# A hybrid decoder layer on one core: a head's norm moved into the next head, value products two steps behind their transposes, and the input norm on VectorE alone

## The chip, the cores and the metric

The kernel runs on one core of a Trainium2 chip, as one launch. The metric is the device time of that core in microseconds (us), taken as the median over the runs of a kernel. A profiled execution gives the trace; its span is the time from the first to the last instruction, and its own device time is a little longer.

## What is computed

One layer over S = 512 rows of D = 2048 float32 numbers. The input is RMS-normalised, multiplied by one wide weight matrix, and its columns feed two branches whose outputs are merged by per-channel gates, projected and added to the input; a last RMS norm follows.

```
xn   = x * rsqrt(mean(x*x) + eps) * norm_w
proj = xn @ w_in                     # queries, keys, values, gates of both branches
# branch 1: HGRN2, 8 heads of 128, o_t = S_t^T q_t
#   S_t = diag(f_t) S_(t-1) + (1 - f_t) i_t^T;  each head's o: rmsnorm(o, hg_norm_w) * silu(z)
# branch 2: native sparse attention, 16 heads of 128 in 4 groups
#   o = g0 * softmax(q kc) vc  +  g1 * softmax(q k_slc) v_slc  +  g2 * softmax(q k_win) v_win
y    = g * (o_hg @ w_branch_hg) + (1 - g) * (o_nsa @ w_branch_nsa)
out  = rmsnorm(x + y @ w_out, final_norm_w)
```

The heads' norm (the mean over the 128 rows of a head, `rmsnorm(o, hg_norm_w)`), the input norm and the attention's weighted sum of values are what the change touches. The compressed keys and values (kc, vc) are 31 blocks per group.

## The kernel before, in words

All large products are three TensorE products in a 32-bit format (`mm3`, lines 139 to 141): each float32 operand is split into a rounded high part and the rest. The split takes one cast on ScalarE and one subtraction on VectorE: `load_w` (lines 130 and 131) for weights that DMAs bring in blocks of 512 KB on SyncE's queue, `split` (lines 135 and 136) for everything computed.

A planner orders each engine's instructions from the written order, with the buffers' reuse as constraints; an engine then runs its queue in that order, and waits where an operand or a buffer isn't ready. `weave(main, n, side, m)` (line 272) interleaves two generators: main yields between the products of a weight matrix, and side steps in proportion m to n.

PSUM, the memory that TensorE writes, has eight banks: three `pj` for projections, two `sc`, two `pt` and one `po`; `lbank` (line 95) takes `sc` and `pt` in turn.

The stages, by their place in the span: the input norm, transposes of x and the first products (0 to 61 us); gate units and column sums (to 125); gates and values (to 475); the eight recurrence heads (475 to 860); the compressed keys and values and the first branch's output (to 1160); the four groups of the sparse attention, NSA (1160 to 1700); the second branch's and the output products (to 2107).

*Input norm.* `normalise(i)` (line 323) takes one of four row tiles: squares of one half on ScalarE (line 329) and of the other on VectorE (line 330), the sum (line 335), root (336), reciprocal (337). Of the four quarters of 512 columns two are scaled and multiplied by the norm's weight in one VectorE operation, STT (line 341: tensor times scalar times tensor); the other two are first multiplied by the weight on GpSimd (line 334) and then scaled on VectorE (line 343). GpSimd also spreads the weight over the partitions (line 305). `transposed` (349) and `first` follow per quarter.

*Recurrence heads.* `hg_proj(h + 1)` is woven with 17 steps of `hg_core(h)` (line 540). The core builds decayed queries and keys by levels of halved blocks: `grow` (line 567) and `decayed` (line 577) on VectorE with a product on GpSimd (566), TensorE's scores (587, 601) and masked copies on VectorE (588, 590, 605). Then transposes of kd (635, copied to kn), state updates (TensorE 644, VectorE 648), the output products in `po` (655, 657), its squares, and at the end the norm: two products with a matrix of 1/128 (668, 669), root (670), reciprocal (671), STT (672), the product with the gate (673), and a store to `ohg_d`.

*NSA groups.* `nsa_proj(g + 1)` (queries, keys, two gate units `z_units`) is woven with `nsa_core(g)` (line 849). The values of a group come from DRAM by two DMAs on ScalarE's queue into a tile of their own, `vraw`, of one buffer (line 822), which is split into vh and vl. `nsa_core` starts with the compressed scores of four heads (copied, transposed at 868, softmaxed in `pc` by lines 876 to 885); `cmp_t` (line 892) transposes the result into pch and pcl. Per head and per block of rows i = 3 to 0 come the scores (in `sc` banks, evacuated by line 921 with mask and maximum), the exponential (925), and the scaling on GpSimd (930). Then, per part, transposes of the probabilities (949), their split into pth and ptl, and the value products of the part before, in `po`.

## Time and profile before

| | |
|---|---|
| median of 3 runs | 2109.39 us (2108.59 to 2112.3) |
| profiled execution, its own time | 2108.82 us |
| its span | 2106.7 us |
| TensorE busy | 98% of the span |
| VectorE busy | 57% |
| ScalarE busy | 39% |
| GpSimd busy | 15% |
| mean granted clock of TensorE | 0.996 |

TensorE's busy share says that it nearly always has a product in its pipeline; it does not say that it starts one at its best pace, since a product that waits a little is hidden behind the one before. What a wait costs is read from the starts of its products and from the table of waits.

### The profile page before, as it was taken

The page shows a single profiled execution, that of the slowest core. Times are in us where ns is not written, and L with a number is a line of the kernel's source. Part 1 is how long each engine was busy: PE and PEld are TensorE (multiplying, and loading weights), DVE is VectorE, ACT ScalarE, POOL GpSimd, SP SyncE. Part 2 cuts the span into 40 slices and gives each one's busy share as a digit, 9 for nine tenths or more (in the row PEclk, how much of TensorE's full clock was granted, in tenths as well). Part 3 has the DMA queues.
Part 4 walks back from the last instruction along what each step waited for, and adds up shares of the span by engine and source line. Part 5 has one row for each costly group of instructions (what it writes and reads, how often), then busy time and mean ns, then how long its engine had stood idle before and what let it go on. Part 6 is the DMA issues. An engine that isn't in the chain of part 4 may idle for free.

```text
span 2106.7 us, 26671 instructions
## 1 busy us (share of the span) xinstructions
PE 2062.0 (98%) x10304; PEld 1721.2 (82%) x10304; DVE 1209.0 (57%) x1875; ACT 816.5 (39%) x1267; POOL 322.4 (15%) x411
## 2 busy tenths in 40 slices
PE   7999999999999999999999999999999999999998
PEld 6888888888888778878888887877878888888887
DVE  7687778745456655566545665657654453433333
ACT  4454444532233233344323444445445432222232
POOL 2000000003233432100002222213212100000000
PEclk9999999999999999999999999999999999999999
DMA  6325243332323222566752222222223394445232
GB/s 184 100 105 180 100 152 114 121 101 74 96 83 93 76 76 85 167 188 202 247 164 85 74 73 85 68 84 64 78 75 92 90 304 132 149 140 212 98 130 90
DMA packets 306595, 254.46 MB, mean 121 GB/s; under 512 B 10666, under 2 KB 263411, under 8 KB 305827
## 3 DMA queue, kind: packets, MB, share of 16 engines
q1 hardware_dynamic: 282980, 202.55, 31.8%
q0 software_dynamic: 8096, 26.28, 3.4%
q10 hardware_dynamic: 15392, 23.92, 3.3%
q8 instruction: 81, 1.33, 0.3%
q14 instruction: 46, 0.38, 0.1%
HBM read 222.25 MB, written 30.47 MB: 120 GB/s over the span
## 4 chain that ended last, share of the span: by engine, by line
PE 82%; DVE 7%; issue 4%; ACT 3%; DMA 3%; POOL 1%; SPq 0%; ACTq 0%; DVEq 0%; POOLq 0%
PE pj L139 17%; PE pj L141 17%; PE pj L140 17%; PE sc L214 4%; PE pt L214 4%; PE sc L215 2%; PE pt L215 2%; PE sc L141 2%; PE sc L139 2%; PE sc L140 2%; PE po L140 1%; DVE whl L131 1%; PE po L139 1%; PE po L141 1%; PE pt L949 1%
## 5 line engine op out<-in xcount | busy, mean ns | idle before, releaser
L139 PE MATMUL pj<-xhl,whl 128*128 128x512 f32 x1344 | 538.5, 401 | 0.0
L141 PE MATMUL pj<-xhl,whl 128*128 128x512 f32 x1344 | 527.7, 393 | 0.8 <-DVE whl L131 0.8
L140 PE MATMUL pj<-xhl,whl 128*128 128x512 f32 x1344 | 525.2, 391 | 0.0
L131 DVE TENSOR_TENSOR whl<-wr,whl 128x1024 fp32r<-128x1024 f32 x244 | 303.8, 1245 | 373.2 <-ACT whl L130 372.5
L130 ACT CAST whl<-wr 128x1024 fp32r<-128x1024 f32 x244 | 256.5, 1052 | 563.3 <-PE pj L141 446.8
L141 PEld LDWEIGHTS pj<-xhl,whl 128*128 128x128 f32 x1344 | 252.3, 188 | 56.6 <-DVE whl L131 2.0
L140 PEld LDWEIGHTS pj<-xhl,whl 128*128 128x128 f32 x1344 | 252.9, 188 | 46.4
L139 PEld LDWEIGHTS pj<-xhl,whl 128*128 128x128 f32 x1344 | 252.7, 188 | 46.1
L135 ACT CAST whl<-xt 128x1024 fp32r<-128x1024 f32 x75 | 78.6, 1052 | 97.7 <-PE pt L215 33.1
L136 DVE TENSOR_TENSOR whl<-xt,whl 128x1024 fp32r<-128x1024 f32 x75 | 91.5, 1223 | 39.3 <-ACT whl L135 39.2
L930 POOL TENSOR_SCALAR s<-s,sm 128x512 f32<-128x512 f32 (+3 forms) x128 | 82.2, 655 | 149.4 <-DVE sm L928 89.9
L139 PE MATMUL pj<-onh,whl 128*128 128x512 f32 x256 | 99.6, 389 | 0.0
L140 PE MATMUL pj<-onl,whl 128*128 128x512 f32 x256 | 99.6, 389 | 0.0
L141 PE MATMUL pj<-onh,whl 128*128 128x512 f32 x256 | 99.6, 389 | 0.0
L136 DVE TENSOR_TENSOR ptl<-pt,pth 128x512 fp32r<-128x512 f32 (+1 forms) x80 | 50.5, 633 | 69.3 <-ACT pth L135 68.6
L925 ACT ACTIVATE s<-s,mx 128x512 f32<-128x512 f32 (+3 forms) x128 | 70.9, 555 | 43.8 <-DVE mx L923 39.0
L135 ACT CAST pth<-pt 128x512 fp32r<-128x512 f32 (+1 forms) x80 | 43.5, 544 | 96.1 <-PE pt L949 95.7
L201 DVE TENSOR_TENSOR xt<-xt 128x1024 f32<-128x1024 f32 x64 | 77.5, 1219 | 0.6
L921 DVE CUSTOM_DVE_ANT_0 s<-sc,cf 128x512 f32<-128x512 f32 (+3 forms) x128 | 59.3, 483 | 20.1 <-PE sc L141 19.4
L698 POOL TENSOR_TENSOR rsh<-rsh,rope 32x512 f32<-32x512 f32 x28 | 42.2, 1507 | 183.8 <-DVE rsh L697 166.3
L566 POOL TENSOR_TENSOR suf<-suf,pre 128x256 f32<-128x256 f32 x56 | 51.8, 926 | 116.7 <-DVE pre L549 94.6
L131 DVE TENSOR_TENSOR cl<-wr,ch 128x1024 fp32r<-128x1024 f32 x32 | 39.1, 1223 | 44.6 <-ACT ch L130 44.6
(431 smaller groups left out, 4004.9 us busy)
## 6 DMA issues: line engine op xcount, KB each, us to landing
wr<-in_w_in_dram SPq DMA_DIRECT2D x172, 512.0 KB
xt<-in_w_in_dram SPq DMA_DIRECT2D x32, 1024.0 KB
wr<-in_w_branch_nsa_dram SPq DMA_DIRECT2D x32, 512.0 KB
wr<-in_w_out_dram SPq DMA_DIRECT2D x32, 512.0 KB
wr<-in_cmp_k_w_dram SPq DMA_DIRECT2D x16, 512.0 KB
wr<-in_w_branch_hg_dram SPq DMA_DIRECT2D x16, 512.0 KB
wr<-in_cmp_v_w_dram SPq DMA_DIRECT2D x16, 512.0 KB
gat_d<-wr POOLq DMA_DIRECT2D x20, 256.0 KB, 3.0
```

The source lines that it names most:

```text
L130: nc.scalar.copy(hi[:, :n], raw[:, :n])
L131: nc.vector.tensor_tensor(lo[:, :n], raw[:, :n], hi[:, :n].bitcast(F32), op=OP.subtract)
L135: nc.scalar.copy(hi, src)
L136: nc.vector.tensor_tensor(lo, src, hi.bitcast(F32), op=OP.subtract)
L139: nc.tensor.matmul(acc, lhsT=lh, rhs=rh, start=start, stop=False, **kw)
L140: nc.tensor.matmul(acc, lhsT=lh, rhs=rl, start=False, stop=False, **kw)
L141: nc.tensor.matmul(acc, lhsT=ll, rhs=rh, start=False, stop=stop, **kw)
L201: nc.vector.tensor_tensor(dst, dst, more, op=OP.add)
L214: nc.tensor.matmul(av, lhsT=l0, rhs=r, start=start, stop=False, skip_group_check=True)
L215: nc.tensor.matmul(av[:, 0], lhsT=l1, rhs=r[:, 0], start=False, stop=stop, skip_group_check=True)
L925: nc.scalar.activation(s[:, b], s[:, b], AF.Exp, scale=SCALE, bias=mx[:, b:b + 1], accum_out=sm[:, b:b + 1])
L930: nc.gpsimd.tensor_scalar(s[:, b], s[:, b], sm[:, b:b + 1], 1.0, op0=OP.mult, op1=OP.mult)
```

## The change

Three edits. In `normalise` all four quarters use the one VectorE operation, and GpSimd's products go. In `hg_core` the norm of a head becomes a function that is kept in a list and run in the next head, after that head's kn; the last head runs its own at its end. In the NSA, the values are loaded in two tiles named `raw` (two buffers, shared with the roped queries and keys, the gate units and the compressed values); the value products wait in a list `due` until two steps after their transposes, and the last two of a head run in the next head's score steps; the first score product of block 2 goes to a `pj` bank; `cmp_t` comes right after the scores of block 1 of the first head; pth384 and ptl384 have two buffers; the weave takes 46 steps and not 48.

```diff
             nc.scalar.activation(sq, x[:, h1], AF.Square, accum_out=ss[:, 1:2])
             nc.vector.scalar_tensor_tensor(sq2, x[:, h0], 1.0, x[:, h0], op0=OP.mult, op1=OP.mult,
                                            accum_out=ss[:, 0:1])
-            for k0 in (8, 12):
-                c = slice(k0 * P, (k0 + 4) * P)
-                nc.gpsimd.tensor_tensor(x[:, c], x[:, c], nw[:, c], op=OP.mult)
             nc.vector.tensor_tensor(ss[:, :1], ss[:, :1], ss[:, 1:], op=OP.add)
             nc.scalar.activation(ss[:, :1], ss[:, :1], AF.Sqrt, scale=1.0 / D, bias=epst)
             nc.vector.reciprocal(ss[:, :1], ss[:, :1])
             for k0 in range(0, KD, 4):
                 c = slice(k0 * P, (k0 + 4) * P)
-                if k0 < 8:
-                    nc.vector.scalar_tensor_tensor(x[:, c], x[:, c], ss[:, :1], nw[:, c], op0=OP.mult, op1=OP.mult)
-                else:
-                    nc.vector.tensor_scalar(x[:, c], x[:, c], ss[:, :1], None, op0=OP.mult)
+                nc.vector.scalar_tensor_tensor(x[:, c], x[:, c], ss[:, :1], nw[:, c], op0=OP.mult, op1=OP.mult)
 
         def transposed(i, k0):
             ts = slice(i * P, (i + 1) * P)
...
     with pool("hg") as hp:
         hgw = sv[:, R_HGW:R_HGW + 1]
         heads = {}
+        left = []
         def values(pr):
 
             vb = [bank() for _ in range(2)]
...
             kn = hp.tile([P, 3 * P], F32, name="kn", bufs=2)
             nc.scalar.copy(kn, ps[:, :3 * P])
             yield
+            if left:
+                left.pop()()
             yield
             ps = lbank()
             st = hp.tile([P, 3, P], F32, name="st", bufs=2)
...
             split(sh, sl, ob)
             yield
             yield
-            pm = lbank()
-            nc.tensor.matmul(pm, lhsT=ones, rhs=sh, start=True, stop=False)
-            nc.tensor.matmul(pm, lhsT=ones, rhs=sl, start=False, stop=True)
-            nc.scalar.activation(ob, pm, AF.Sqrt, bias=epst)
-            nc.vector.reciprocal(ob, ob)
-            nc.vector.scalar_tensor_tensor(ow, ow, hgw, ob, op0=OP.mult, op1=OP.mult)
-            nc.vector.tensor_tensor(ow, ow, zs, op=OP.mult)
-            nc.gpsimd.dma_start(ohg_d[head], ow)
+
+            def normed():
+                pm = lbank()
+                nc.tensor.matmul(pm, lhsT=ones, rhs=sh, start=True, stop=False)
+                nc.tensor.matmul(pm, lhsT=ones, rhs=sl, start=False, stop=True)
+                nc.scalar.activation(ob, pm, AF.Sqrt, bias=epst)
+                nc.vector.reciprocal(ob, ob)
+                nc.vector.scalar_tensor_tensor(ow, ow, hgw, ob, op0=OP.mult, op1=OP.mult)
+                nc.vector.tensor_tensor(ow, ow, zs, op=OP.mult)
+                nc.gpsimd.dma_start(ohg_d[head], ow)
+
+            left.append(normed)
+            if head == HG - 1:
+                left.pop()()
 
         weave(hg_proj(0), 0)
         for head in range(HG - 1):
...
     gv5 = gt.rearrange("p i (g h b) -> p i g h b", g=GROUPS, b=3)
 
     def nsa_proj(g):
-        raw = ap.tile([P, 4, 2, DH], F32, name="vraw")
-        for b in range(2):
-            nc.scalar.dma_start(raw[:, :, b], v_d[1 + b, :, :, g * DH:(g + 1) * DH].rearrange("i p c -> p i c"))
         vh = ap.tile([P, 4, 2, DH], F32R, name="vh", bufs=2)
         vl = ap.tile([P, 4, 2, DH], F32R, name="vl", bufs=2)
-        f = lambda t: t.rearrange("p j e c -> p (j e c)")
-        split(f(vh), f(vl), f(raw))
+        for b in range(2):
+            raw = ap.tile([P, S], F32, name="raw", bufs=2)
+            rv = raw.rearrange("p (i c) -> p i c", i=4)
+            nc.scalar.dma_start(rv, v_d[1 + b, :, :, g * DH:(g + 1) * DH].rearrange("i p c -> p i c"))
+            split(vh[:, :, b], vl[:, :, b], rv)
         q = []
         for h in range(HPG):
             acc = bank()
...
         p3h = ap.tile([P, 2, HPG, P], F32R, name="p3h")
         p3l = ap.tile([P, 2, HPG, P], F32R, name="p3l")
         o3 = ap.tile([P, HPG, P], F32, name="o3")
+        due = []
+
+        def pv_next():
+
+            if not due:
+                return
+            h, po, parts, hi, lo, last = due.pop(0)
+            for n, (j, b) in enumerate(parts):
+                w = slice(n * (4 - j) * P, (n + 1) * (4 - j) * P)
+                mm3(po[:, j * P:], vh[:, j, b], vl[:, j, b], hi[:, w], lo[:, w], False, last)
+            if last:
+                ow = ap.tile([P, 384], F32, name="ow", bufs=2)
+                nc.vector.tensor_copy(ow, po[:, :384])
+                nc.scalar.copy(o3[:, h], po[:, 384:])
+                nc.gpsimd.dma_start(ons_d[g * HPG + h][:, :384], ow)
+
         for h in range(HPG):
             qh, ql = q[h]
             sc = {}
...
                 s = sc[i] = ap.tile([P, 2, n], F32, name=f"s{i}", bufs=1)
                 mx = ap.tile([P, 2], F32, name="mx", bufs=4)
                 sm = ap.tile([P, 2], F32, name="sm", bufs=4)
+                if i > 1:
+                    pv_next()
                 if i < 2:
                     ps = sbank()
                     pv = ps[:, :2 * n].rearrange("p (b k) -> p b k", b=2)
...
                 else:
                     pb = []
                     for b in range(2):
-                        ps = sbank()
+                        ps = bank() if i == 2 and b == 0 else sbank()
                         mm3(ps[:, :n], qh[:, qs], ql[:, qs], kh[:, b, :n], kl[:, b, :n], True, True)
                         pb.append(ps[:, :n])
                 mk = causal[:, 3 - i:].rearrange("p j k -> p (j k)")
...
                 nc.vector.tensor_tensor(sm, sm, gv[:, i, h, 1:3], op=OP.mult)
                 for b in range(2):
                     nc.gpsimd.tensor_scalar(s[:, b], s[:, b], sm[:, b:b + 1], 1.0, op0=OP.mult, op1=OP.mult)
+                if h == 0 and i == 1:
+                    cmp_t()
                 yield
-            if h == 0:
-                cmp_t()
-                yield
-            po = psum("po")
-            mm3(po, vcz[0][:, h], vcz[1][:, h], ph, pl, True, False)
-            pend = None
-
-            def pv_mm(parts, hi, lo, last):
-                for n, (j, b) in enumerate(parts):
-                    w = slice(n * (4 - j) * P, (n + 1) * (4 - j) * P)
-                    mm3(po[:, j * P:], vh[:, j, b], vl[:, j, b], hi[:, w], lo[:, w], False, last)
-
-            for parts in (((3, 0), (3, 1)), ((2, 0), (2, 1)), ((1, 0),), ((0, 0),), ((1, 1),), ((0, 1),)):
+            for m, parts in enumerate((((3, 0), (3, 1)), ((2, 0), (2, 1)), ((1, 0),), ((0, 0),), ((1, 1),), ((0, 1),))):
                 ps = tbank()
                 o = 0
                 for j, b in parts:
...
                     pv = ps[:, :o].rearrange("p (b k) -> p b k", b=2)
                     split(p3h[:, :, h], p3l[:, :, h], pv)
                 else:
-                    hi = ap.tile([P, o], F32R, name=f"pth{o}", bufs=o // 256)
-                    lo = ap.tile([P, o], F32R, name=f"ptl{o}", bufs=o // 256)
+                    hi = ap.tile([P, o], F32R, name=f"pth{o}", bufs=2)
+                    lo = ap.tile([P, o], F32R, name=f"ptl{o}", bufs=2)
                     split(hi, lo, ps[:, :o])
-                    if pend:
-                        pv_mm(*pend, False)
-                    pend = (parts, hi, lo)
+                    if m == 2:
+                        po = psum("po")
+                        mm3(po, vcz[0][:, h], vcz[1][:, h], ph, pl, True, False)
+                    elif m > 2:
+                        pv_next()
+                    due.append([h, None, parts, hi, lo, m == 5])
+                    if m >= 2:
+                        for d in due:
+                            d[1] = po
                 yield
-            pv_mm(*pend, True)
-            ow = ap.tile([P, 384], F32, name="ow", bufs=2)
-            nc.vector.tensor_copy(ow, po[:, :384])
-            nc.scalar.copy(o3[:, h], po[:, 384:])
-            nc.gpsimd.dma_start(ons_d[g * HPG + h][:, :384], ow)
+        while due:
             yield
+            pv_next()
+        yield
 
         ps = sbank()
         for b in range(2):
...
 
     weave(nsa_proj(0), 0)
     for g in range(GROUPS - 1):
-        weave(nsa_proj(g + 1), 128, nsa_core(g), 48)
+        weave(nsa_proj(g + 1), 128, nsa_core(g), 46)
     
     def last():
         yield from z_units(14, 16, ap, "raw")
         yield from merge_gates(NG, NG + 6, ap, "raw")
 
-    weave(last(), 112, nsa_core(GROUPS - 1), 48)
+    weave(last(), 112, nsa_core(GROUPS - 1), 46)
     nsa.close()
 
 
```

The planner's order shows where the pieces come to lie. First VectorE at the start, before and then after (xt is x, wfl the low part of the first weight, xhl the split x):

```order
L341 SCALAR_TENSOR_TENSOR xt<-xt,ss,nw 128x512 x2
L131 TENSOR_TENSOR wfl<-wraw,wfh 128x1216
L136 TENSOR_TENSOR xhl<-pt,xhl 128x4x128
L131 TENSOR_TENSOR wfl<-wraw,wfh 128x1216
L136 TENSOR_TENSOR xhl<-sc,xhl 128x4x128
L330 SCALAR_TENSOR_TENSOR sq_269,ss<-xt 128x1024
L343 TENSOR_SCALAR xt<-xt,ss 128x512 x2
L335 TENSOR_TENSOR ss<-ss 128x1
L337 RECIPROCAL ss<-ss 128x1
```

```order
L337 SCALAR_TENSOR_TENSOR xt<-xt,ss,nw 128x512 x4
L131 TENSOR_TENSOR wfl<-wraw,wfh 128x1216
L136 TENSOR_TENSOR xhl<-pt,xhl 128x4x128
L131 TENSOR_TENSOR wfl<-wraw,wfh 128x1216
L136 TENSOR_TENSOR xhl<-sc,xhl 128x4x128
L136 TENSOR_TENSOR xhl<-pt,xhl 128x4x128
L136 TENSOR_TENSOR xhl<-sc,xhl 128x4x128
L330 SCALAR_TENSOR_TENSOR sq_267,ss<-xt 128x1024
L332 TENSOR_TENSOR ss<-ss 128x1
```

All four quarters of the first tile are scaled before the first weight's subtraction; two splits of x follow the second weight without another row tile between them.

Second VectorE at the end of a head's state updates, from those updates to the next head's first ones: before, and then after (st is the state, ob and ow the norm's tiles, ad the scores, zs the gate):

```order
L648 SCALAR_TENSOR_TENSOR st<-st,pre,sc 128x128 x2
L131 TENSOR_TENSOR whl<-wr,whl 128x1024 x2
L537 TENSOR_TENSOR zs<-pj,zs 128x512
L136 TENSOR_TENSOR sl<-ob,sh 128x512
L131 TENSOR_TENSOR whl<-wr,whl 128x1024 x2
L547 TENSOR_SCALAR kt<-sg,nomlb,omlb 128x512
L549 TENSOR_SCALAR pre<-sg,omlb,lbt 128x512
L552 TENSOR_TENSOR qf<-qf,pre 128x4x64
L671 RECIPROCAL ob<-ob 128x512
L567 TENSOR_TENSOR pre<-pre 128x256
L131 TENSOR_TENSOR whl<-wr,whl 128x1024
L672 SCALAR_TENSOR_TENSOR ow<-ow,sv,ob 128x512
```

```order
L620 TENSOR_TENSOR qd<-qf,pre 128x384
L600 COPY_PREDICATED ad<-cm,sc 128x16x16
L131 TENSOR_TENSOR whl<-wr,whl 128x1024 x2
L670 RECIPROCAL ob<-ob 128x512
L131 TENSOR_TENSOR whl<-wr,whl 128x1024
L671 SCALAR_TENSOR_TENSOR ow<-ow,sv,ob 128x512
L645 SCALAR_TENSOR_TENSOR st<-st,pre,sc 128x128
L672 TENSOR_TENSOR ow<-ow,zs 128x512
L645 SCALAR_TENSOR_TENSOR st<-st,pre,sc 128x128
L532 TENSOR_TENSOR zs<-pj,zs 128x512
```

The reciprocal, STT and product have moved from ahead of the next head's `pre`, `qk` and masked copies to between the qd product, the scores' last copy and the state updates.

Third ScalarE at the start of an NSA group (group 1), before and then after:

```order
L135 CAST vh<-vraw 128x1024
L130 CAST whl<-wr 128x1024
L178 ACTIVATE raw<-pj 128x512
L822 DMA vraw<-v_d 128x4x128
L855 DMA raw<-vc_d 31x128 x4
L864 COPY pc<-sc 128x512
L822 DMA vraw<-v_d 128x4x128
L135 CAST vczh<-raw 128x512
L879 ACT_TABLE_LOAD
L879 ACTIVATE pc<-pc 128x512
```

```order
L130 CAST whl<-wr 128x1024
L178 ACTIVATE raw<-pj 128x512
L828 DMA raw<-v_d 128x4x128
L135 CAST vh<-raw 128x4x128
L867 COPY pc<-sc 128x512
L828 DMA raw<-v_d 128x4x128
L858 DMA raw<-vc_d 31x128 x4
L135 CAST vh<-raw 128x4x128
L882 ACT_TABLE_LOAD
L882 ACTIVATE pc<-pc 128x512
```

The two loads of the values now stand ahead of and behind the copy of the compressed scores, the cast of each half comes right behind, and the exponential stands behind the second cast.

## Rows read from the trace of the kernel before

**Rows 1.** Page, busy time: us, share of span, instructions; first engine.

```profile
PE 2062.0 (98%) x10304; PEld 1721.2 (82%) x10304; DVE 1209.0 (57%) x1875; ACT 816.5 (39%) x1267; POOL 322.4 (15%) x411
```

**Rows 2.** Timeline of TensorE, 584 to 591 us: start, us, line, shape; first and last.

```profile
584.16 0.40 PE L139 MATMUL pj<-xhl,whl 128*128 128x512 f32 x1
...
590.08 0.39 PE L141 MATMUL pj<-xhl,whl 128*128 128x512 f32 x1
```

**Rows 3.** Waits of TensorE, whole span: waited for, us, times, longest.

```profile
PE sc L139 <- DVE mx L921: 8.9, 6, 2.5
PE sc L601 <- DVE ad L605: 7.4, 7, 1.3
...
PE pt L349 <- issue: 3.4, 2, 1.8
PE pt L349 <- DVE xt L343: 1.7, 1, 1.7
...
PE po L140 <- DVE ptl L136: 1.6, 3, 0.5
```

**Rows 4.** Busy time by stretch: length, us busy (instructions), clock, DMA share, GB/s.

```profile
25.50:28.80 3.30, 3.30 (x13) 2.76 (x13) 3.30 (x4) 3.30 (x6) 0.00 (x0) 0.50 0.44 136
30.00:60.00 30.00, 26.85 (x189) 25.08 (x189) 29.54 (x39) 14.25 (x25) 6.33 (x5) 1.00 0.31 83
```

**Rows 5.** Groups by line, GpSimd, 0 to 62 us: busy, mean ns, idle before.

```profile
L334 POOL TENSOR_TENSOR xt<-xt,nw 128x512 f32<-128x512 f32 x8 | 11.6, 1472 | 15.8 <-issue 7.4 <-ACT sq L329 5.6 <-DMA wr<-in_w_in_dram 2.7
```

**Rows 6.** Groups by line and shape, VectorE, 0 to 62 us.

```profile
L343 DVE TENSOR_SCALAR xt<-xt,ss 128x512 f32<-128x512 f32 x8 | 7.5, 974 | 1.9 <-POOL xt L334 1.9
L341 DVE SCALAR_TENSOR_TENSOR xt<-xt,ss,nw 128x512 f32<-128x512 f32 x8 | 5.9, 768 | 2.7 <-POOL nw L305 2.7
...
L335 DVE TENSOR_TENSOR ss<-ss 128x1 f32<-128x1 f32 x4 | 3.7, 925 | 1.7 <-ACT sq L329 1.5
...
L337 DVE RECIPROCAL ss<-ss 128x1 f32<-128x1 f32 x4 | 0.6, 158 | 0.7 <-ACT ss L336 0.7
```

**Rows 7.** Timeline of VectorE, 583 to 602 us: start, us, line.

```profile
598.47 0.72 DVE L605 COPY_PREDICATED ad<-cm,sc 128x256 f32<-128x256 uint8 x1
```

**Rows 8.** Groups by line and shape, VectorE, 475 to 860 us.

```profile
L671 DVE RECIPROCAL ob<-ob 128x512 f32<-128x512 f32 x8 | 26.8, 3346 | 0.7 <-ACT ob L670 0.7
L672 DVE SCALAR_TENSOR_TENSOR ow<-ow,sv,ob 128x512 f32<-128x512 f32 x8 | 9.5, 1192 | 0.0
...
L673 DVE TENSOR_TENSOR ow<-ow,zs 128x512 f32<-128x512 f32 x8 | 6.0, 747 | 0.0
L648 DVE SCALAR_TENSOR_TENSOR st<-st,pre,sc 128x128 f32<-128x128 f32 x16 | 5.6, 348 | 22.3 <-PE sc L644 22.3
```

**Rows 9.** Groups by line and shape, ScalarE, 475 to 860 us.

```profile
L130 ACT CAST whl<-wr 128x1024 fp32r<-128x1024 f32 x55 | 57.8, 1051 | 186.9 <-PE pj L141 186.7
...
L670 ACT ACTIVATE ob<-pt,epst 128x512 f32<-128x512 f32 x8 | 5.5, 691 | 0.1
```

**Rows 10.** Timeline of TensorE, 1291 to 1297 us.

```profile
1295.66 0.60 PE L892 MATMUL pt<-ident,pc 128*128 128x128 f32 x4
```

**Rows 11.** Timeline of VectorE, 1270 to 1294 us.

```profile
1292.00 0.86 DVE L885 TENSOR_TENSOR pc<-pc,cst 128x512 f32<-128x512 f32 x1
```

**Rows 12.** Timeline of ScalarE, 1270 to 1294 us.

```profile
1274.27 0.39 ACTq L822 DMA_DIRECT2D vraw<-v_d  x1
...
1285.44 1.28 ACT L879 ACT_TABLE_LOAD   x1 [2.20 <-DVE pc L878]
1286.73 0.63 ACT L879 ACTIVATE pc<-pc 128x512 f32<-128x512 f32 x1
```

**Rows 13.** Timeline of GpSimd, 1272 to 1292 us.

```profile
1276.27 0.54 POOL L180 DMA_DIRECT2D z_d<-raw  x1 [1.76 <-DVE raw L179]
```

**Rows 14.** DMA issues, 1274 to 1278 us: KB each, us to landing.

```profile
z_d<-raw POOLq DMA_DIRECT2D x1, 256.0 KB, 6.0
```

**Rows 15.** DMA issues of the whole span: KB each, median us to landing.

```profile
v_d<-wr POOLq DMA_DIRECT2D x12, 256.0 KB, 3.5
```

## The prediction

> **What bounds the kernel now.** I read the page first: TensorE is busy 2062.0 of 2106.7 us [rows 1], so a change can only win what TensorE loses between its instructions. A 128x512 product starts every 0.228 us when nothing is in its way (26 steps from 584.16 to 590.08 [rows 2]), and this change neither removes nor adds products for TensorE. So the question is which waits go and which come. The table of TensorE's waits over the whole span [rows 3] gives the candidates; the three edits lie at three places in it, and at each I then read the rows of the engines that are waited for.
>
> - First stage (0 to 62 us). TensorE loses 3.4 us at two transposes of x for which the table names no engine and 1.7 for the scaling of x at line 343 [rows 3]. VectorE is busy 29.54 of the 30 us from 30 to 60 [rows 4]: here it is the bound. GpSimd makes it worse. Its multiplies start 7.4 us late for nothing that the profile shows [rows 5], and while they run VectorE is slow: eight scalings of line 343 take 974 ns in the mean, four one-column adds of line 335 take 925 [rows 6]. The clock is granted at 0.50 (1.2 of 2.4 GHz) from 25.5 to 28.8 [rows 4].
> - Recurrence heads (475 to 860 us). TensorE waits 7.4 us, seven times, at line 601 for the masked copy of line 605 [rows 3]. In the second head that copy starts only at 598.47 [rows 7], since the reciprocal, the scaled product and the product with the gate (3346, 1192 and 747 ns [rows 8]) of the head before stand ahead of it in VectorE's queue. Counted as TensorE's starts against its pace, the seven cost 9.3 us (the table's 7.4 is plain idle time).
> - NSA groups (1140 to 1700 us). TensorE waits 8.9 us in six places for the evacuation of score banks and 1.6 us for the low part of transposed probabilities, ptl [rows 3]. Against its pace I count 11.5 us at the four group starts (0.95, 3.65, 2.95, 3.95) and 2.6 at ptl.
>
> **The change part by part.**
>
> Input norm. Eight scalings of line 343 and eight GpSimd multiplies go; eight more of line 341's operation (STT) come. The scalings take 7.5 us in all; eight STT take 5.9 in all now [rows 6], so 5.9 more. The adds of line 335 take 3.7 us for four and, with GpSimd quiet, should take what the one-column reciprocal takes, 158 ns each [rows 6]: 3.1 less. VectorE also sits idle 1.9 us until GpSimd is done [rows 6]. That is 1.6 + 3.1 + 1.9 = 6.6 us in a stage that VectorE bounds. Against it, the subtraction of the first weight part stands behind two more STT, 1.5 us later; the third part comes earlier, since its cast stands on ScalarE behind a root that waits for a held-up add. I take 5.0 us gained. Bounds: 1 (if the first weight part's delay and a slow clock eat most) and 6.7 (the waits 3.4 + 1.7 [rows 3] and 1.6 for the slow clock, half of 3.3). GpSimd's switch of 7.4 us [rows 5] now falls ahead of its first product of the recurrence stage; between its last work before and that product it has some 24 us of nothing to do, so I cost it at nothing. Without that cover the first head would start as much later.
> Only the means over both states stand in the rows: an STT at 768 ns, a scaling at 974 [rows 6]. The Trainium skill (VectorE: DVE Perf Modes, Mode 2×_2P) says the opposite of fp32: one tensor with a scalar can use both read ports, two tensors cannot, so that the scaling should be the shorter. By that rule alone a scaling takes half of 768 ns and the edit costs VectorE eight times 0.38 us, a loss of 3.1 and not a gain of 1.6. I go by the rows, which have GpSimd beside it.
>
> Late norm of a head. Two products, root, reciprocal, STT, product and the store of ohg_d move from the end of a head to the next one's kn step. The store stays on GpSimd's queue, and nobody reads it before the branch product. The 9.3 us at line 601 should go: without 5.3 us of work (3.35 + 1.19 + 0.75 [rows 8]) ahead of it, the copy is done before TensorE asks. But the moved work now stands ahead of the state updates of line 648 (the second order below: reciprocal, a weight subtraction, STT, one update, product, the other update). Counted from the transposes of kd: products of ones after 2.3 us, root done at 3.1 (0.69 [rows 9]), reciprocal to 6.5; the weight subtraction waits for a cast (1.05 [rows 9]) behind TensorE's last product of a weight block at 6.5, so it runs from 7.5 to 8.7; STT to 9.4 (0.74 when nothing slows it, the nearest being the product's 0.75), first update 0.35 [rows 8] to 9.75. TensorE reaches the product that reads it after 36 products at 0.228 and ten small ones at about 0.1: 9.2. It waits 0.6 us, and 0.5 more for the second update behind the product of 0.75. That is 1.1 us in each of six heads (2 to 7, whose order is the same), 6.6 us. Taken: 9.3 - 6.6 = 2.7 gained. Bounds: 0 (1.5 a head, STT at its mean of 1.19) and 9.3 (no new wait).
>
> NSA. Value products run two steps behind their transposes, so ptl is no longer waited for: 2.6 us gained. The second buffers of pth384 and ptl384, and the bank of the other kind for one score product, cost TensorE nothing: they only take waits away. Two things cost. First, the transposes of the compressed probabilities (cmp_t, line 892) come 12 TensorE instructions earlier. Now they start at 1295.66 [rows 10], after two waits of 3.65 us in all; without waits TensorE would be there at 1292.0, and 12 instructions sooner at 1289.4, while pc is finished at 1292.86 (1292.00 + 0.86 [rows 11]). So TensorE waits 3.4 us even with pc as early as today: the wait changes its name. Second, the load of the values loses its own buffer. Today it is issued at 1274.27 [rows 12], a whole group ahead of its use. After the change its second half shares two buffers with the gate unit, whose store is issued at 1276.27 [rows 13] and lands 6.0 us later [rows 14], at 1282.3. Then come the load (3.5, the median of the stores to v_d of its size [rows 15]), a cast (about 0.6, half of a 128x1024 one [rows 9]), the table load (1.28) and the exponential, at 1287.7; it starts at 1286.73 now [rows 12]. ScalarE's queue holds the exponential behind that cast (third order below), VectorE's five steps on pc hang on it, and TensorE on them. So 3.4 + 0.9 = 4.3 us at each of four starts, 17.2 against 11.5: 5.7 lost, with ptl 3.1 lost. Bounds: 9.1 lost (5.8 each, the load landing 1.5 later) and 14.1 gained (all waits gone: 11.5 + 2.6).
>
> Sum: 5.0 + 2.7 - 3.1 = 4.6 us gained, 2108.82 to 2104.2 for the profiled execution. The median of the runs shown is 0.57 above that execution: **2104.8 us**.
>
> **The rivals.**
> 1. All waits at the group starts go, and the new one in the heads does not show. For it: TensorE's total wait at ptl and sc is there to be won, the loads may be early enough, and the weight cast in the heads hangs on a buffer that may come free sooner. Against it: pc is late today as well [rows 11]. 5.0 + 9.3 + up to 14.1; with half of the last 21.3: 2088. A milder form (new head waits gone, NSA even) gives 14.3: 2095.
> 2. No gain at the start. TensorE has to wait 1.4 us more for the first weight part and some for the next x tiles, and a wait may bring the clock to 0.50 as from 25.5 to 28.8 [rows 4], at 1.7 us. Then 0 + 2.7 - 3.1: 2109.8, no change. The rule above of the Trainium skill (VectorE: DVE Perf Modes, Mode 2×_2P) would lead here.
> 3. Slower: the second half of the values, behind the gate unit's store, holds ScalarE's queue longer. With the load taking 6.0 us (as the store [rows 14]) and not 3.5, the wait is 6.8 each, 27.2: NSA loses 13.1, and 5.0 + 2.7 - 13.1 = -5.4 gives 2114.8. It decides from 6.5 us a start on.
> 4. The change does not do what it says: the planner could put the pieces back where they were. The orders below exclude it.
>
> **How the numbers follow.** The forecast and its neighbours (gains of 0 to 9) have 0.58; rival 1 has 0.20, rival 2 0.12, rival 3 0.10. A measurement of this kernel can tell about 0.2% (4.2 us) from no change, so faster is below 2105.2. Of the forecast's 0.58 a little over half lies beyond it; with rival 1 that makes faster 0.50. Rival 2 and the rest of the forecast make the same 0.38, and rival 3 with a little of rival 2 slower 0.12. The ends of the sum, which need every bound at once: all low, 1 + 0 - 9.1, 2117.5; all high, 6.7 + 9.3 + 14.1, 2079. The range leaves out the far parts of rivals 1 and 3: 2094 to 2113.
>
> **What would show it.** Right: no wait of line 343 in the first stage and the last first-stage product some 5 us earlier than now; no wait at line 601 for line 605; in its place one before the products that read st, about 1 us a head; waits of about 4 us a group start before the transposes of pc, released by the last step on pc, and none for ptl. Wrong: the value load's second half not behind the store, TensorE not stopping at st, or the clock at half for longer in the first stage.

## The result

The changed kernel takes 2085.81 us in the median of four runs (2082.91 to 2087.46), and the one before 2108.99 on the same occasions: a ratio of 0.9887, with a 95% interval of 0.9869 to 0.9905. That is 23 us, 1.1%, where 4.6 us were forecast. The profiled execution took 2082.91 us at a span of 2081.1.

The page of the changed kernel, busy time (before: [rows 1]):

```profile
span 2081.1 us, 26681 instructions
...
PE 2052.0 (99%) x10304; PEld 1721.8 (83%) x10304; DVE 1203.1 (58%) x1879; ACT 812.2 (39%) x1271; POOL 309.6 (15%) x403
```

TensorE issues the same 10304 instructions in 25.6 us less span. Its waits in the changed kernel, whole span (before: [rows 3]): what is waited for, us, times, longest.

```profile
PE pt L895 <- DVE mx L944: 4.6, 4, 1.7
PE pt L343 <- DVE xt L337: 3.8, 1, 3.8
...
PE pj L139 <- ACT wfh L130: 1.7, 1, 1.7
...
PE sc L139 <- DVE mx L942: 1.1, 1, 1.1
...
PE pt L871 <- ACT pc L867: 0.8, 1, 0.8
...
PE pj L140 <- DVE wfl L131: 0.7, 1, 0.7
```

The waits at the heads' scores (7.4 us) are gone, and none before the products with the state has come. The score banks' 8.9 us are 1.1; the transposes of pc (now line 895) wait 4.6 us in all and not in each group 4.3. ptl is no longer listed. At the start TensorE waits for the third weight part, first for its cast and then for its subtraction (1.7 and 0.7 us), and hardly for later quarters of x.

To compare stages I counted TensorE's starts against its pace: each interval between two of its products, less what that product takes when nothing is in the way (0.2275 us for 512 columns, 0.174 for 384, 0.1395 for 304, 0.1175 for 256, about 0.11 for a small float32 instruction). What is left is lost time, shorter gaps and slow clock included. The stages are cut at the same progress of TensorE's work. The differences sum to 25.8, the spans differ by 25.6. The compressed keys' stage varies from 5.6 to 8.6 over all kernels below whatever their edit, so its 1.6 is not put down to the change.

| us lost in | before | changed | difference |
|---|---|---|---|
| first stage | 20.9 | 13.2 | -7.7 |
| the other three stages | 10.2 | 10.1 | -0.1 |
| recurrence heads | 13.1 | 4.1 | -9.0 |
| compressed keys, first branch | 6.1 | 7.6 | +1.6 |
| NSA groups | 22.3 | 11.7 | -10.6 |

So the heads gave 9.0 where 2.7 were forecast, the NSA gave 10.6 where a loss of 3.1 was forecast, and the first stage somewhat more than its 5.0. Each column of the table is one execution; e1_norm below, which has the same first stage, loses 15.1 us there and not 13.2.

### The profile page after: what moved, and what is told of

Its sections match the earlier page's. It is cut to its first block, busy times and chain, and to the rows that moved or that the text cites. A ratio compares the mean times of both kernels' runs of the same rounds, so it can differ in the third digit from the quotient of the medians.

```text
span 2081.1 us, 26681 instructions
## 1 busy us (share of the span) xinstructions
PE 2052.0 (99%) x10304; PEld 1721.8 (83%) x10304; DVE 1203.1 (58%) x1879; ACT 812.2 (39%) x1271; POOL 309.6 (15%) x403
## 4 chain that ended last, share of the span: by engine, by line
PE 87%; issue 5%; DVE 4%; DMA 2%; ACT 1%; POOL 1%; ACTq 0%; SPq 0%; DVEq 0%; POOLq 0%
PE pj L139 18%; PE pj L141 18%; PE pj L140 18%; PE sc L214 4%; PE pt L214 4%; PE sc L215 2%; PE pt L215 2%; PE sc L141 2%; PE sc L140 2%; PE sc L139 2%; PE po L139 1%; PE pt L960 1%; PE po L141 1%; PE po L140 1%; PE pj L214 1%
## 5 line engine op out<-in xcount | busy, mean ns | idle before, releaser
L701 POOL TENSOR_TENSOR rsh<-rsh,rope 32x512 f32<-32x512 f32 x28 | 48.5, 1731 | 141.8 <-DVE rsh L700 132.8
L942 DVE CUSTOM_DVE_ANT_0 s<-sc,cf 128x512 f32<-128x512 f32 (+3 forms) x112 | 50.8, 475 | 29.0 <-PE sc L141 25.1
L561 POOL TENSOR_TENSOR suf<-suf,pre 128x256 f32<-128x256 f32 x56 | 45.9, 820 | 80.8 <-DVE pre L544 75.0
```

## The experiments

All but the change were timed in five rounds beside the kernel before, and the change on its own occasions beside it; ratios are to the kernel before, and kernels are compared by them. The gain in us is the difference from 1 times 2110.

| kernel | median us | ratio (95%) | gain, us |
|---|---|---|---|
| the change | 2085.81 | 0.9887 (0.9869 to 0.9905) | 23.8 |
| e1_norm: input norm alone | 2105.8 | 0.9970 (0.9959 to 0.9982) | 6.3 |
| e2_late: late norm alone | 2103.06 | 0.9963 (0.9951 to 0.9976) | 7.8 |
| e3_nsa: NSA edits alone | 2100.96 | 0.9952 (0.9938 to 0.9965) | 10.1 |
| e4_vcz: compressed values early alone | 2099.74 | 0.9939 (0.9926 to 0.9951) | 12.9 |
| n6_vload: values' loads alone | 2105.55 | 0.9973 (0.9962 to 0.9983) | 5.7 |
| n2_cmp: change, cmp_t as before | 2083.69 | 0.9871 (0.9858 to 0.9884) | 27.2 |
| n3_allvcz: change, compressed values early | 2082.27 | 0.9865 (0.9852 to 0.9878) | 28.5 |
| n4_e124: e1, e2 and e4 | 2084.36 | 0.9876 (0.9864 to 0.9889) | 26.2 |
| n8_bank: change, all scores in sc | 2084.73 | 0.9878 (0.9864 to 0.9892) | 25.7 |
| n9_pv1: change, value products one or no step behind | 2095.97 | 0.9932 (0.9920 to 0.9945) | 14.3 |
| n7_best: n3 and n2 together | 2081.5 | 0.9865 (0.9849 to 0.9880) | 28.5 |

### The three edits one at a time

**e1_norm** has the diff's first part (in `normalise`) alone.

> The kernel before with the input norm's edit alone. Theory A (three edits that add up, each at its own place): 7 to 8 us faster, TensorE's losses before 62 us 13 in place of 21, none after that changed. Theory B (the stage was VectorE's, and only VectorE's saved time counts): 4 to 5 us. Rival (what the first stage gains is given back, since the next stages wait for the same DMAs): 0 to 2 us.

It is 6.3 us faster (3.8 to 8.7), between the two theories, and the interval holds both. By its profile the first stage loses 15.1 in place of 20.9 us. In that one execution two later stages lose about 1.5 and 1.2 us more than in the kernel before; there the granted clock is lower for a while (0.79 in the mean from 892 to 900 us and 0.83 from 1552 to 1562, where it was 1.00 before). What brought it down is not shown. Waits of TensorE in e1_norm that belong to the first stage:

```profile
PE pt L343 <- DVE xt L337: 2.9, 1, 2.9
PE pj L139 <- ACT wfh L130: 2.0, 1, 2.0
...
PE pj L140 <- DVE wfl L131: 1.1, 2, 0.7
```

The first tile's transposes still wait (it is the DMA and the norm itself); the waits for weight parts, 3.1 us, are new. Only 0.5 of them stand at the first part's subtraction, which the prediction had 1.5 us later. The other 2.7 (2.0 for the cast, 0.7 for the subtraction) stand at the third part. It does come earlier, as the prediction had it, but TensorE is ready for it earlier still.

**e2_late** has the diff's second part (in `hg_core`) alone.

> The kernel before with the heads' late norm alone. Theory A: the wait at line 601 goes and no wait comes in its place, because the small float32 products take two instructions each and TensorE comes to the state later than the prediction had it: 9 us faster. The prediction's theory (1.1 us of new wait a head): 2 to 3 us. Rival: the gain needs the other edits: under 1 us.

It is 7.8 us faster (5.1 to 10.3). The prediction's figure of 2 to 3 is outside, theory A's 9 inside. No wait at line 601's products nor at the state products is left in its list; the heads lose 5.5 us in place of 13.1. Its profiled execution, at 2106.99 us, is the longest of its five; later stages lose more in it, again with the granted clock below 1.00 (0.79 from 892 to 900 us).

**e3_nsa** has the rest of the diff alone.

> The kernel before with the NSA edits alone. Theory A: 9 to 11 us faster, the four group starts left with waits of 1 to 2 us before the transposes of pc. The prediction's theory: 3 us slower. Rival (most of it comes from a shifted start of the stage in the full change): 3 to 6 us.

It is 10.1 us faster (7.4 to 13.1), as theory A had it. Its waits in the NSA stage:

```profile
PE pt L892 <- DVE mx L941: 3.4, 4, 1.5
PE sc L139 <- DVE mx L939: 2.3, 1, 2.3
```

The three gains add up: 6.3 + 7.8 + 10.1 = 24.2 against 23.8 for the whole, within intervals of some 2.5 us each. By the waits, each part works at its own place.

### What the NSA edits gained from

At a group start of the kernel before, VectorE's timeline (start, us, line; in brackets the idle time before and its releaser) shows a row that I had not read:

```profile
1278.89 0.69 DVE L876 TENSOR_TENSOR pc<-pt,cf 128x512 f32<-128x512 f32 x1 [2.92 <-PE pt L868]
1283.32 0.69 DVE L136 TENSOR_TENSOR vczl<-raw,vczh 128x512 fp32r<-128x512 f32 x1 [3.74 <-ACT vczh L135]
1283.93 0.68 DVE L877 TENSOR_REDUCE cst<-pc 128x16 f32<-128x512 f32 x1
```

The split of the compressed values, vczl, stands between the first two steps on pc and waits 3.74 us for a cast (vczh, on ScalarE) that waits for its DMA. All later steps on pc, and the score evacuations of line 921 behind them, waited with it. This is the second group; in the third and fourth vczl stands ahead of every step on pc, and in the first it waits for nothing. Over the four, VectorE's waits for that cast are:

```profile
DVE vczl L136 <- ACT vczh L135: 16.5, 3, 6.9
```

In the changed kernel the same stretch reads:

```profile
1262.10 0.69 DVE L879 TENSOR_TENSOR pc<-pt,cf 128x512 f32<-128x512 f32 x1 [1.65 <-PE pt L871]
1262.82 0.69 DVE L880 TENSOR_REDUCE cst<-pc 128x16 f32<-128x512 f32 x1
...
1270.31 0.68 DVE L136 TENSOR_TENSOR vczl<-raw,vczh 128x512 fp32r<-128x512 f32 x1
```

Here vczl comes after the sum over pc (its second reduction), and waits for nothing. So it is in the first three groups. In the last one vczl still stands ahead of pc's steps and waits 6.0 us for its cast, and the wait at the transposes of pc is the longest of the four there (1.7 us).

**e4_vcz** takes that wait away from the kernel before by loading earlier: the tile, its clearing and its four DMAs go from the start of `nsa_core(g)` into `nsa_proj(g)`, behind the second query. To make room the output tile `ow` has one buffer.

```diff
             q.append((qh, ql))
+            if h == 1:
+                vcr[g] = ap.tile([P, S], F32, name="vcr", bufs=1)
+                nc.gpsimd.memset(vcr[g], 0.0)
+                for n in range(HPG):
+                    nc.scalar.dma_start(vcr[g][n * 32:n * 32 + NC, n * DH:(n + 1) * DH], vc_d[g * NC:(g + 1) * NC, :])
...
-        raw = ap.tile([P, S], F32, name="raw", bufs=2)
-        nc.gpsimd.memset(raw, 0.0)
-        for h in range(HPG):
-            nc.scalar.dma_start(raw[h * 32:h * 32 + NC, h * DH:(h + 1) * DH], vc_d[g * NC:(g + 1) * NC, :])
+        raw = vcr[g]
...
-            ow = ap.tile([P, 384], F32, name="ow", bufs=2)
+            ow = ap.tile([P, 384], F32, name="ow", bufs=1)
```

> The kernel before with one thing changed: the compressed values are loaded a group ahead into a buffer of their own (ow has one buffer for that), so their split no longer stands between the steps on pc in VectorE's queue and waits for no DMA there. Theory C (at the group starts of the kernel before, VectorE's steps on pc and the score evacuations behind them waited for that DMA, and the change's gain there is that its split of vcz falls behind them): 6 to 9 us faster, the score waits of 8.9 us down to under 3. Rival D (the gain comes from the value products' two steps, the bank and the earlier cmp_t): under 2 us, the score waits as before.

It is 12.9 us faster (10.3 to 15.6), more than theory C asked, and no less than the whole of the NSA edits. Waits of TensorE in its NSA stage:

```profile
PE po L139 <- ACT pth L135: 2.4, 3, 0.9
PE sc L139 <- DVE mx L924: 0.4, 1, 0.4
```

The score waits went from 8.9 to 0.4 us. So the wait for the compressed values' DMA was what the group starts of the kernel before paid for. Rival D falls as an account of those waits. Two things stay untold apart. The cast, vczh, stood in ScalarE's queue ahead of the exponential on pc just as vczl stood in VectorE's, and e4 moves both. And e4 gives the tile a buffer of its own and takes its clearing on GpSimd away from the group start, besides loading it earlier.

**n6_vload** takes only the values' loads from the change (`nsa_proj` of the diff). In VectorE's order vczl then stands behind the sum over pc in three of four groups.

> The kernel before with the loads of the values alone taken from the NSA edits (two raw tiles in place of vraw); the value products, the banks and cmp_t stay. In VectorE's order the split of vcz now stands behind the first sum over pc in three of the four groups. Theory C (that place in the queue is what the change gained at the group starts): 5 to 8 us faster, score waits of about 3 us, most of them at the last group, where the split stays ahead. Rival D (value products, bank and cmp_t): 0 to 2 us. The prediction's view of the loads: 2 to 4 us slower.

It is 5.7 us faster (3.6 to 8.0), and its score waits are 4.6 in place of 8.9:

```profile
PE sc L139 <- DVE mx L921: 4.6, 3, 2.9
PE po L140 <- DVE ptl L136: 1.6, 3, 0.5
```

So the loads, which the prediction charged as a loss, bring about half of the 10.1 or more (3.6 to 8.0), and the planner's new place for vczl is the difference that shows. The fourth group's order keeps vczl ahead, and the longest wait, 2.9, fits it. ptl is waited for as before.

**n9_pv1** was meant to put the value products back to one step behind, the rest as in the change:

```diff
+                    if m == 2:
+                        pv_next()
+                        pv_next()
+                    if m == 5:
+                        pv_next()
```

> The changed kernel with the value products one step behind their transposes and a head's last one at its own end, as before the change. Theory F (the two steps carry the part of the NSA gain that the loads don't, of which 2.6 us are the waits for ptl): 3 to 6 us slower than the changed kernel, with waits before value products for pth or ptl. Rival E (the bank): 0 to 2 us slower.

It gains 14.3 (11.6 to 16.9) and not 23.8: 9.5 us slower than the change, more than theory F had. Its waits in the NSA stage:

```profile
PE po L140 <- DVE ptl L136: 4.2, 6, 1.0
PE pt L895 <- DVE mx L944: 2.8, 4, 1.3
PE po L139 <- ACT pth L135: 0.9, 3, 0.3
```

Value products wait 5.1 us in nine places. By the count of starts the stage loses 20.7 us and not 11.7, and the value products alone some 9.6 more than in the change.

But the edit does not restore what was there before. At m = 2 it takes two entries from the list, and the second is the part whose transposes have just been written; at m = 5 it does the same. Of a head's five parts these two stand no step behind, where the kernel before had a step between with products of the weights in it. TensorE in n9_pv1, and below it the same part of a head in the kernel before:

```profile
1317.14 0.49 PE L960 MATMUL pt<-ident,s 128*128 128x128 f32 x3
...
1318.88 0.34 PE L139 MATMUL po<-pth,vh 128*128 128x384 f32 x1
1319.58 0.44 PE L140 MATMUL po<-ptl,vh 128*128 128x384 f32 x1 [0.35 <-DVE ptl L136]
```

```profile
1303.18 0.49 PE L949 MATMUL pt<-ident,s 128*128 128x128 f32 x3
...
1305.95 0.43 PE L139 MATMUL po<-pth,vh 128*128 128x384 f32 x1
```

In the median over the sixteen heads, the first value product of these two parts starts 1.5 and 1.0 us after the last transpose's start in n9_pv1, 3.4 and 2.4 us in the kernel before, 5.7 and 6.9 in the change. So n9_pv1 shows what no step costs, and does not measure one step against two. One step against two, with the early load in both, is n4_e124 against n3_allvcz below.

**n8_bank** and **n2_cmp** undo one small part each:

```diff
-                        ps = bank() if i == 2 and b == 0 else sbank()
+                        ps = sbank()
```

> The changed kernel with the first score product of block 2 back in an sc bank. Theory C: score banks are waited for only where VectorE is late, and that is mostly gone: 0 to 2 us slower than the changed kernel (21 to 23 faster than before). Rival E (the bank of the other kind carries the part of the NSA gain that the loads don't): 4 to 6 us slower than the changed kernel.

```diff
-                if h == 0 and i == 1:
-                    cmp_t()
                 yield
+            if h == 0:
+                cmp_t()
+                yield
```

> The changed kernel with cmp_t back behind the scores of the first head, a step of its own. Theory C: the wait of 4.6 us at the transposes of pc goes and comes back as smaller waits at the score banks: 0 to 3 us faster than the changed kernel, so 23 to 26 faster than before. Rival D (the earlier transposes are part of the gain): 2 to 5 us slower than the changed kernel.

Neither differs from the change by more than the intervals (0.9878 and 0.9871 against 0.9887). Rival E falls: the bank carries nothing that can be told in the time, though without it the waits move (2.9 us at the score banks, 0.3 at the transposes of pc). The early cmp_t is no gain either; without it the 4.6 us before the transposes of pc go and 3.0 come at the transposes of the probabilities. Whether it costs a little stays open.

### Versions beyond the change

**n4_e124** has e1, e2 and e4 and none of the NSA edits; **n3_allvcz** is the change with e4's load; **n7_best** is n3 with cmp_t as before.

> The kernel before with the input norm's edit, the late norm and the early compressed values, and none of the NSA edits. Theory A (parts add up): 5.5 + 8.3 + 11.6 = 25.4 us faster than before, 2 faster than the changed kernel. Rival (the parts share waits): 18 to 22 us.

> The changed kernel with the compressed values loaded a group ahead into a buffer of their own (ow with one buffer). Theory C: pc's steps are free of that DMA in the changed kernel already but for the last group, so 0 to 2 us faster than the changed kernel (23 to 25 faster than before). Rival (ScalarE's queue of loads and casts still sets pc): 3 to 5 us faster than the changed kernel.

> The changed kernel with the compressed values loaded a group ahead and cmp_t back behind the scores of the first head. Theory C: the waits at the transposes of pc (1.7 us left with the early load) go, so 1 to 3 us faster than with the early load alone, 29 to 32 faster than before. Rival (what is left is at pc's copy and at GpSimd's scaling, which neither edit touches): no faster than the early load alone.

n4 gains 26.2 (23.4 to 28.7), with theory A: one early load of 62 KB a group does what the whole NSA part did, with the value products one step behind. What the NSA edits, two steps among them, add once the load is early is n3 against n4: 2.3 us by the ratios, and not told from nothing. n3 gains 28.5 (25.7 to 31.2) and n7 28.5 (25.3 to 31.9). By their medians they are 3.5 and 4.3 us below the change, and the upper ends of their intervals reach into its own, so that they are faster than the change is likely and not shown. n7 is not told from n3, which is its rival's outcome. Both beat the kernel before by more than the change's median gain.

## Why the prediction was wrong

**What bounds the kernel** was right: all gain came from TensorE's waits at the three places named, and the first rival's outcome (waits at the group starts mostly go, the new one in the heads doesn't show) is what happened. Its reasons were not: in the heads the weight's cast came when the forecast had it, and for the group starts the rival names no vczl. Its figure of 2088 took half of the waits in the heads and the NSA as gone, and 2085.81 was measured; that it lies so near is in part luck. I gave it 0.20 and let the range end above it.

**Input norm: right in the main.** 5.0 forecast, 6.3 measured alone (3.8 to 8.7). The rows of VectorE in the first stage of the changed kernel [rows 6], by line and shape:

```profile
L337 DVE SCALAR_TENSOR_TENSOR xt<-xt,ss,nw 128x512 f32<-128x512 f32 x16 | 11.2, 748 | 0.2
```

Sixteen operations take 11.2 us where eight of each kind took 7.5 + 5.9 = 13.4, and the 1.9 us of waiting for GpSimd are gone. The one-column adds were sized too high: the four take 1.8 us where 3.7 were spent, so 1.9 less and not 3.1, since the first still stands beside the spreading of the norm's weight. In this stage the clock was not at half again after 18.5 us, as it had been from 25.5 to 28.8 [rows 4]; stretches of the changed kernel (length, busy us of TensorE, weights, VectorE, ScalarE and GpSimd, clock, DMA share, GB/s):

```profile
22.00:26.00 4.00, 3.12 (x21) 2.72 (x21) 4.00 (x5) 2.84 (x4) 0.00 (x0) 1.00 0.86 292
26.00:30.00 4.00, 3.97 (x30) 3.73 (x29) 3.41 (x8) 2.38 (x7) 0.27 (x1) 1.00 0.61 161
```

GpSimd's late start cost nothing that shows: the largest single loss left in the recurrence stage is 0.22 us, by the count of starts.

The rule on the scaling (the Trainium skill, VectorE: DVE Perf Modes, Mode 2×_2P) speaks of VectorE alone. In the kernel before, the scaling took, on VectorE's timeline, with GpSimd's multiplies beside it and without them:

```profile
19.93 2.88 DVE L343 TENSOR_SCALAR xt<-xt,ss 128x512 f32<-128x512 f32 x2 [1.88 <-POOL xt L334]
...
41.38 0.47 DVE L343 TENSOR_SCALAR xt<-xt,ss 128x512 f32<-128x512 f32 x1
```

1.44 us each against 0.47, while the operation that replaced it takes 0.75 on the average. So the shorter instruction was the longer one here. That GpSimd shares its interfaces to SBUF, the memory of these tiles, with VectorE, and contends with VectorE's instructions in a two-port mode or with two inputs there, is stated by the Trainium skill (GPSIMD Engine Reference, 8. Key points); the two rows agree with it.

**Late norm: the step that failed is "ten small ones at about 0.1: 9.2".** VectorE's part of the working held. Its timeline in the changed kernel, one head:

```profile
692.00 3.35 DVE L670 RECIPROCAL ob<-ob 128x512 f32<-128x512 f32 x1 [1.26 <-ACT ob L669]
696.40 1.23 DVE L131 TENSOR_TENSOR whl<-wr,whl 128x1024 fp32r<-128x1024 f32 x1 [1.04 <-ACT whl L130]
697.54 0.75 DVE L671 SCALAR_TENSOR_TENSOR ow<-ow,sv,ob 128x512 f32<-128x512 f32 x1
698.20 0.34 DVE L645 SCALAR_TENSOR_TENSOR st<-st,pre,sc 128x128 f32<-128x128 f32 x1
...
699.39 0.35 DVE L645 SCALAR_TENSOR_TENSOR st<-st,pre,sc 128x128 f32<-128x128 f32 x1 [0.24 <-PE sc L641]
```

and TensorE's:

```profile
688.89 0.49 PE L630 MATMUL sc<-ident,kd 128*128 128x128 f32 x3
...
693.12 0.38 PE L641 MATMUL sc<-vt,kn 128*128 128x128 f32 x2
...
697.85 0.61 PE L652 MATMUL po<-ad,vt 128*128 128x128 f32 x4
698.29 0.39 PE L654 MATMUL po<-qd,st 128*128 128x128 f32 x2
...
699.19 0.39 PE L654 MATMUL po<-qd,st 128*128 128x128 f32 x2
...
699.86 0.41 PE L654 MATMUL po<-qd,st 128*128 128x128 f32 x2
```

Counted from 688.89, the first update ends at 9.65 (9.75 forecast). TensorE comes to the product that reads it at 10.30 and not at 9.2, 0.65 us after the update and not 0.5 before it. Each plain float32 product of 128x128 is two instructions (x2 stands where the order has one), and I had counted one; the 128x128 transposes are one each. That is seven instructions more, 0.8 us of the 1.1 that TensorE came later; the rest lies in the first 512-column product behind float32 ones, which takes 0.31 us to the next start (689.14 to 689.45) and not 0.23. The trace of the kernel before tells it by a count, had I asked for the line (durations min, median, max, then first and last start): three products a head, 24 in eight heads, stand as x48.

```profile
L657 PE MATMUL po<-qd,st x48: 275/275/275, 513.1 to 844.0; 128*128 128x128 f32 x48
```

The second update ends at 699.74 and is read at 699.86: a margin of 0.12 us.

**NSA: two steps failed.** "So TensorE waits 3.4 us even with pc as early as today" took pc's time from the kernel before without asking what it waited for. TensorE's own place was right: in the group that the prediction reads, the second, it came to the transposes of pc 11.9 us after the end of the copy of the compressed scores, where the forecast has 11.8 (1289.4 less 1277.59). But from the end of that copy to the end of the last step on pc it took 15.3 us before (1277.59 to 1292.86 [rows 11]) and 13.1 after (1260.79 to 1273.90), now that vczl and its DMA no longer stand in between; 16.2 were forecast. The third order ahead of the prediction shows ScalarE's side of that move: vczh stands ahead of the exponential before, and no longer after. The prediction read from it only the new cast that had come. And "its second half shares two buffers with the gate unit" named the wrong buffer. ScalarE's timeline in the changed kernel:

```profile
1260.20 0.59 ACT L867 COPY pc<-sc 128x512 f32<-128x512 f32 x1 [0.48 <-PE sc L141]
1260.48 0.38 ACTq L828 DMA_DIRECT2D raw<-v_d  x1
1263.87 1.34 ACTq L858 DMA_DIRECT2D raw<-vc_d  x4
1265.25 0.62 ACT L135 CAST vh<-raw 128x512 fp32r<-128x512 f32 x1 [4.46 <-issue]
1265.89 1.28 ACT L882 ACT_TABLE_LOAD   x1
1267.18 0.63 ACT L882 ACTIVATE pc<-pc 128x512 f32<-128x512 f32 x1
```

The second half is issued at 1260.48, right when the first half's buffer is free (its subtraction ran from 1259.76 for 0.69); the gate unit's store went out at 1259.31, and it is GpSimd's clearing of the tile for the compressed values that waited for it, until 1263.31. Behind that clearing ScalarE's queue holds the four loads of the compressed values, issued from 1263.87 to 1265.21, and right behind them the cast, as the third order has them. So the store does hold the exponential, by another way than forecast and for less: the cast at 1265.25 comes 5.9 us after that store's issue, where 9.5 (6.0 + 3.5) were charged. What was right is the name of the new wait. TensorE now stands before the transposes of pc, 1.40 us in this group:

```profile
1274.05 0.63 PE L895 MATMUL pt<-ident,pc 128*128 128x128 f32 x4 [1.40 <-DVE mx L944]
```

It is 4.6 us over four groups and not 17.2; and ptl's waits went, as forecast.

Of the signs named, three came as said (no wait of line 343; no wait at line 601, now 596; none for ptl). Two did not (a wait of about 1 us a head; waits of 4 us at the group starts). The last first-stage product starts at 55.33 us, 5.8 earlier.

## What to carry to other kernels

When an engine's queue holds a split of freshly loaded data between two steps of a chain, look at what that split waits for before costing anything else in the chain: one early load of 62 KB a group was worth as much here as a rewritten schedule. And an experiment that undoes one part of a change has to be read in the trace as well: n9_pv1 was to go back to one step, and went back to none in two parts of five. And where the order of the changed kernel is at hand, follow each instruction that changed its place on every engine, not only on the one where the new wait is suspected. A margin of under a microsecond must be counted in instructions as the trace has them: a product in the code may be two.

## What was not expected of the hardware

A one-column add takes 0.16 us alone; in the changed kernel the first one, at 9.12 us, still took 1.34 while GpSimd was spreading the norm's weight over the partitions, and in the kernel before the four took 0.93 in the mean [rows 6]. So the spreading of the weight, and not only the multiplies, goes with a slow add. Not every VectorE instruction was longer beside GpSimd: in the kernel before, the squares at 36.20 (128x1024) took 1.21 us, as the 1.22 at 16.83 without GpSimd, and there the two multiplies of GpSimd took 3.57 us together, where the two at 29.55 took 2.71.
